# Input stage of a hybrid S5 and forgetting-attention block: norm weights spread by TensorE, memory's copies placed ahead of x's squares, one weight load moved forward

## The chip, the cores and the metric

The kernel runs on one core of one Trainium2 chip. The time is the device time of one execution in microseconds (us). A core has a matrix engine (TensorE, PE in the profile; its weight loads are PEld), VectorE (DVE), ScalarE (ACT), GpSimd (POOL) and SyncE (SP), which here only issues DMA transfers. Each engine runs its own instructions in a fixed order and waits on semaphores for the others. Tiles lie in SBUF (128 partitions); matrix products land in eight PSUM banks of 128x512 float32.

## What is computed

One decoder block over 1024 tokens of width 1024, with 256 memory tokens. The part that the change touches is the start: the normalised input, the normalised memory, its keys and values, and the first 512 columns of the input projection.

```python
def rms_norm(x, gain):
    xf = x.astype(jnp.float32)
    y = xf * lax.rsqrt(jnp.mean(xf * xf, axis=-1, keepdims=True) + RMS_EPS)
    return (y * gain.astype(jnp.float32)).astype(x.dtype)
...
    u = rms_norm(h, norm_mix[l])
    proj = u @ w_in[l]
    u_ssm, q, k, v, f_logit, gate_logits = jnp.split(proj, [...], axis=-1)
...
    # in the cross-attention
    k, v = jnp.split(rms_norm(mem, norm_mem_kv[l]) @ w_kv, 2, axis=-1)
```

After that come the state-space branch, forgetting attention, the gates, an output projection, the cross-attention, a SwiGLU FFN and a final norm. None of that code is changed.

## The kernel before

Every product is made in three passes of a fast float32 format: each operand is split into a high part (a cast copy on ACT, line 177) and a low part (source minus high part, line 178, on VectorE or for a few weights on GpSimd). `mm3` (lines 167 to 169) then runs high x high, high x low, low x high.

`stage_in` treats two memory tiles (`m`, `n`) and eight x tiles (`0` to `7`) of 128 tokens, and twelve weight pieces of 512 KB: 0 to 3 for the memory's keys, 4 to 7 for its values, 8 to 11 for the 512 columns of u. Its order is written out by hand in the string `ORDER_IN`, one short word a step; a scheduler then sets each engine's own order, starting from that string. The words:

- `F` loads a tile, `G` loads a norm weight spread over 128 partitions, `Q` squares a tile on ACT with a row sum, `R` makes the reciprocal root (VectorE, one power on GpSimd, VectorE), `S` scales the tile by root and norm weight on VectorE (`S3g`: ACT and GpSimd).
- `T` turns half a tile on TensorE into a PSUM bank (line 222), `E` copies the turned half out, split into high (`mh` or `uh`, ACT) and low (`ml` or `ul`, VectorE).
- `D` loads a weight piece (hexadecimal number), `W` splits it (`g`: low part on GpSimd), `K` and `V` are keys and values, `U` and `u` a product for u and its copy out, `Z` stores keys and values, `L` issues the small loads of the state-space parameters, `P` prepares these parameters, `X` issues that many warm-up products.

Three things in it matter for what follows. The turned halves use one bank of `misc` and two of `pv`, so a `misc` half can be turned only after the half before it has been copied out, both parts. The raw weights have few buffers (two `raw`, one `xraw`; the u pieces `wr` take tiles of the `xt` ring, that is of x tiles already turned), so a load can wait on SP for a split, and all loads behind it wait too. And ACT does squares, high parts and PSUM copies in one queue.

The norm weight comes in by one transfer that writes it to all partitions:

```python
    def gains(i):
        gain[i] = xtile("gain")
        S.dma_start(gain[i], (g_kv if i == 0 else g_mix).partition_broadcast(P))
```

Of the kernel before, what the change touches and what calls it, by code (L numbers as in the profile page):

```python
# [9 lines left out]
F32 = mybir.dt.float32  # L10
# [3 lines left out]
AF = mybir.ActivationFunctionType  # L14
# [5 lines left out]
P = 128  # L20
D = 1024
# [17 lines left out]
RSLOT_LATE = (0, 1, 2, 3, 4, 4, 5, 5, 6, 6, 7, 7)  # L39

ORDER_IN = """
G0 Fm Qm Fn D1 X60 Qn Rm D0 Sm F1 G1 Tm0 Rn Em0 Sn Tn0 F0 D2 Tm1 W0 Q0 Tn1 En0 F2 F3 D3 Q1 W1g En1 Em1 K0 F4 F5 K1 R0
S0 T00 T01 k0 E00 Q2 W2g D4 F6 F7 D8 E01 S1 T10 Q3 W3 k1 D5 K3 K2 W4 E10 W5 D6 R1 k2 T11 k3 S2 Q4 V0 S3g T30
E11 D7 Q5 T20 R2 T21 E21 E20 S4 E30 W6 D9 W7 T40 V1 S5 E40 T31 V2 E31 W8 T41 V3 Da Z0 L0 T50 Q6 v T51 W9
E51 U00 Db Z2 Q7 E41 R3 S6 u00 L1 Wa T60 E50 S7 T61 T70 Wbg E61 U10 E60 T71 E70 E71 P0 U20 u10 u20 P1 U21 U11 U30
P2 u30 U31 u11 u31 U01 u21 P3 P4 P5 u01
"""

# [18 lines left out]
def f32(ap):  # L67
    return ap.bitcast(F32)
# [50 lines left out]
class Block:  # L119
# [54 lines left out]
            self.mm3(ps, wh[:, k0 + k, :], wl[:, k0 + k, :], rh, rl, k == 0, k == nk - 1)  # L174

    def split(self, hi, lo, src, pool_lo=False):
        self.A.copy(hi, src)  # L177
        (self.G if pool_lo else self.V).tensor_sub(lo, src, f32(hi))  # L178

    def rstd(self, src):  # L180
# [111 lines left out]
def hybrid_block_kernel(ctx: ExitStack, tc: tile.TileContext, x, mem, norm_mix, w_in, b_forget,  # L292
# [22 lines left out]
    with tc.tile_pool(name="ssm", bufs=1) as sp:  # L315
        s5 = S5(B, sp, lam_re[0], lam_im[0], log_dt[0], b_re[0], b_im[0], c_re[0], c_im[0], d_skip[0])
        with tc.tile_pool(name="xin", bufs=1) as xp:
            stage_in(B, xp, s5, x, mem, norm_mix[0], norm_mem_kv[0], w_in, w_mem_kv, uT, u_d, kv_d)
        with tc.tile_pool(name="qp", bufs=1, reuse_waits="tile") as qp:
            stage_ssm(B, s5, qp, uT, w_in, gate_d, u_d, y_d, w_mix_out, sums_d)  # L320
# [13 lines left out]
def stage_in(B, xp, s5, x, mem, g_mix, g_kv, w_in, w_mem_kv, uT, u_d, kv_d):  # L334
# [5 lines left out]
    V, A, T, S, small = B.V, B.A, B.T, B.S, B.small  # L340
    junk = xp.tile([P, D], BF16, name="junk")
    mT = Act(xp, "mT", 4, 8, ML, kg=4, name="m")
    tiles, gain, ss, rs, raw, w, ps, us, kv = {}, {}, {}, {}, {}, {}, {}, [], []
    names = {"m": -2, "n": -1, **{str(t): t for t in range(NT)}}

    def xtile(name="xt"):
        return xp.tile([P, D], F32, tag="xt", bufs=12, name=name)

    def fetch(t):
        tiles[t] = xtile()  # L350
        S.dma_start(tiles[t], mem[(t + 2) * P:(t + 3) * P, :] if t < 0 else x[t * P:(t + 1) * P, :])

    def gains(i):
        gain[i] = xtile("gain")
        S.dma_start(gain[i], (g_kv if i == 0 else g_mix).partition_broadcast(P))

    def square(t):
        if t % 2 == 0:
            ss[t // 2] = small.tile([P, 2], F32, name="ss2")
        A.activation(junk, tiles[t], AF.Square, scale=1.0 / 32, accum_out=ss[t // 2][:, t % 2:t % 2 + 1])  # L360

    def root(i):
        rs[i] = B.rsqrt(ss[-1][:, i % 2:i % 2 + 1] if i < 0 else ss[i])
# [4 lines left out]
        B.norm_scale(tiles[t], tiles[t], r, gain[0 if t < 0 else 1], pool=pool)  # L368

    def turn(t, b):  # L370
        ps[t, b] = B.turn(tiles[t], b, ("misc", "pv")[b])

    def evac(t, b):
        B.turned(ps.pop((t, b)), b, *((mT, t + 2) if t < 0 else (uT, t)))
# [58 lines left out]
    def ssm_out(q, h):  # L433
# [4 lines left out]
        if h == 1:  # L438
            S.dma_start(u_d[q].rearrange("t p c -> p t c"), uv)

    prep = s5.prepare()

    acts = {"F": lambda a: fetch(names[a]), "G": lambda a: gains(int(a)), "Q": lambda a: square(names[a]),
            "R": lambda a: root(names[a]),
            "S": lambda a: scale(names[a[0]], a[1:] == "g"),
            "T": lambda a: turn(names[a[0]], int(a[1])), "E": lambda a: evac(names[a[0]], int(a[1])),
            "D": lambda a: wget(int(a, 16)), "W": lambda a: wsplit(int(a[0], 16), a[1:] == "g"),
            "K": lambda a: keys(int(a)), "k": lambda a: keys_out(int(a)), "V": lambda a: values(int(a)),
# [1461 lines left out]
```

## Time and profile before

| what | value |
|---|---|
| time, median of 3 runs | 1594.67 us |
| lowest and highest | 1586.8 and 1595.77 us |
| profiled execution, its own time | 1598.0 us |
| its span, first to last instruction | 1596.3 us |
| mean granted TensorE clock | 0.98 |
| bytes moved by DMA | 258.70 MB |

The profile shows one execution. Its page gives busy time by engine; other views of the same trace show one engine's instructions in order of time (start, duration, engine, line, operation, output<-input, count, and in brackets how long the engine had been idle and what ended that), the sum of waits by pair, and busy times in chosen stretches. An instruction of the memory stage is found by its line and tile names. The profiled execution is 3.3 us above the median of the runs.

### The profile page before, as it was taken

Reading aid. Unit: us, or ns where it says so; the run is one execution under the profiler, and the core shown is the slowest. Engines: PE = TensorE matmul, PEld = TensorE weight load, DVE = VectorE, ACT = ScalarE, POOL = GpSimd, SP = SyncE. Lnnn points to the kernel's source line nnn. Section 1 sums busy time; section 2 is a strip of 40 time slices with the busy share of each in tenths; the row PEclk is TensorE's granted clock in tenths of the full one; section 3 lists DMA queues with packets and bytes.
Section 4 is the critical chain, followed back from the end, with each engine's and each line's share of the span. In section 5 each row is a group of like instructions: output and inputs, shape, how many; then the busy total and the mean of one; then the engine's idle time right before and its main releaser. Section 6 shows DMA issues by size and latency. Waiting matters only on the chain.

```text
span 1596.3 us, 20515 instructions
## 1 busy us (share of the span) xinstructions
PE 1533.6 (96%) x7301; PEld 1261.0 (79%) x7301; DVE 1057.9 (66%) x1892; ACT 678.7 (43%) x1199; POOL 243.6 (15%) x323
## 2 busy tenths in 40 slices
PE   5899999999999899989999999999999999899997
PEld 5688888898777668878888778888888888688886
DVE  5756566444688676769765688677777775465455
ACT  5422334422566553434445564333333333244342
POOL 3015443200121123310002200000000000000001
PEclk8899999999999999999999999999999999999999
DMA  8745556752022736757531186544455544696542
GB/s 268 147 94 92 168 159 163 181 178 30 11 58 45 179 83 207 261 199 275 178 117 56 53 297 247 168 152 152 159 165 161 162 159 165 235 388 218 189 157 106
DMA packets 202870, 258.70 MB, mean 162 GB/s; under 512 B 36024, under 2 KB 127064, under 8 KB 202256
## 3 DMA queue, kind: packets, MB, share of 16 engines
q1 hardware_dynamic: 196144, 241.67, 50.5%
q10 hardware_dynamic: 6624, 15.73, 2.6%
q8 instruction: 57, 0.93, 0.2%
q14 instruction: 45, 0.37, 0.1%
HBM read 176.08 MB, written 83.20 MB: 162 GB/s over the span
## 4 chain that ended last, share of the span: by engine, by line
PE 72%; DVE 10%; DMA 8%; issue 3%; POOL 3%; ACT 3%; SPq 1%; DVEq 0%; ACTq 0%; POOLq 0%
PE mm L964 15%; PE pv L964 7%; PE mm L167 6%; PE mm L168 6%; PE mm L169 6%; PE mm L1101 4%; PE sc L964 4%; PE sc L1101 3%; PE pv L1101 3%; PE sc L167 2%; PE sc L169 2%; PE sc L168 2%; DMA or<-in_w_ffn_out_dram 1%; PE misc L1101 1%; DMA gb<-gate_d 1%
## 5 line engine op out<-in xcount | busy, mean ns | idle before, releaser
L178 DVE TENSOR_TENSOR wlo<-raw,whi 128x1024 fp32r<-128x1024 f32 (+2 forms) x126 | 133.7, 1063 | 104.7 <-ACT whi L177 104.2
L177 ACT CAST whi<-raw 128x1024 fp32r<-128x1024 f32 (+2 forms) x127 | 115.6, 914 | 140.8 <-PE mm L168 36.0
L167 PE MATMUL mm<-uh,whi 128*128 128x512 f32 x344 | 138.7, 403 | 2.2 <-ACT whi L177 2.2
L169 PE MATMUL mm<-uh,wlo 128*128 128x512 f32 x344 | 136.5, 397 | 0.2 <-DVE wlo L178 0.2
L178 DVE TENSOR_TENSOR ol<-or,oh 128x1024 fp32r<-128x1024 f32 x73 | 89.3, 1224 | 71.2 <-ACT oh L177 70.2
L168 PE MATMUL mm<-ul,whi 128*128 128x512 f32 x344 | 136.4, 397 | 0.0
L177 ACT CAST oh<-or 128x1024 fp32r<-128x1024 f32 x73 | 76.8, 1052 | 104.4 <-PE mm L1101 33.6
L996 POOL TENSOR_TENSOR g<-a,c 128x512 f32<-128x512 f32 x22 | 35.6, 1619 | 398.2 <-ACT a L995 398.2
L167 PEld LDWEIGHTS mm<-uh,whi 128*128 128x128 f32 x344 | 65.9, 192 | 14.8 <-ACT whi L177 2.6
L169 PEld LDWEIGHTS mm<-uh,wlo 128*128 128x128 f32 x344 | 65.6, 191 | 15.0 <-DVE wlo L178 1.4
L1729 POOL TENSOR_TENSOR pl<-pf,ph 128x512 fp32r<-128x512 f32 (+1 forms) x32 | 39.7, 1241 | 246.0 <-DVE ph L1728 200.4
L196 POOL TENSOR_TENSOR r<-ms,mhalf 128x1 f32<-128x1 f32 (+1 forms) x30 | 17.9, 599 | 376.9 <-DVE ms L192 347.4
L168 PEld LDWEIGHTS mm<-ul,whi 128*128 128x128 f32 x344 | 65.8, 191 | 11.0
L1726 ACT ACTIVATE pf<-sc 128x512 f32<-128x512 f32 (+1 forms) x96 | 46.5, 490 | 50.0 <-DVE sc L1722 30.4
L964 PE MATMUL pv<-S3h,we 128*128 128x512 f32 x176 | 58.1, 389 | 0.0
L1199 POOL TENSOR_TENSOR sg<-sg,ga 128x512 f32<-128x512 f32 x16 | 33.2, 2102 | 74.1 <-DVE sg L1192 30.1
L1732 DVE TENSOR_TENSOR pl<-pf,ph 128x512 fp32r<-128x512 f32 (+2 forms) x64 | 35.6, 557 | 11.6 <-ACT ph L1731 10.5
L1101 PE MATMUL mm<-oh 128*128 128x512 f32 x106 | 41.2, 389 | 0.0
L1101 PE MATMUL mm<-ol,oh 128*128 128x512 f32 x106 | 41.2, 389 | 0.0
L1101 PE MATMUL mm<-oh,ol 128*128 128x512 f32 x106 | 41.2, 389 | 0.0
L167 PE MATMUL mm<-yh,whi 128*128 128x512 f32 x104 | 41.1, 395 | 0.0
L169 PE MATMUL mm<-yh,wlo 128*128 128x512 f32 x104 | 40.9, 393 | 0.0
(681 smaller groups left out, 4589.5 us busy)
## 6 DMA issues: line engine op xcount, KB each, us to landing
or<-c_d SPq DMA_DIRECT2D x77, 256.0 KB
wo<-in_w_ffn_out_dram SPq DMA_DIRECT2D x22, 512.0 KB
c_d<-g SPq DMA_DIRECT2D x44, 256.0 KB
t_d<-wo SPq DMA_DIRECT2D x44, 256.0 KB
or<-t_d SPq DMA_DIRECT2D x44, 256.0 KB
raw<-in_w_ffn_in_dram SPq DMA_DIRECT2D x20, 512.0 KB
rawb<-in_w_ffn_in_dram SPq DMA_DIRECT2D x20, 512.0 KB
raw<-in_w_in_dram SPq DMA_DIRECT2D x18, 512.0 KB
```

Of the source, the lines that this page charges most:

```text
L167: T.matmul(ps, lh, rh, start=first, stop=False)
L168: T.matmul(ps, lh, rl, start=False, stop=False)
L169: T.matmul(ps, ll, rh, start=False, stop=last)
L177: self.A.copy(hi, src)
L178: (self.G if pool_lo else self.V).tensor_sub(lo, src, f32(hi))
L964: T.matmul(ps, l_[:, k, :], r_, start=first and k == 0 and i == 0, stop=k == 3 and i == 2, skip_group_check=True)
L996: G.tensor_mul(g[:, 512:], a1, c1)
L1101: T.matmul(ps, l_[:, gi], r_[:, 512:], start=n < 3 and p == 0 and k == 0 or n == 7 and p == 0 and k == 0, stop=p == NP - 1 and k == 2, ski ...
L1199: self.B.G.tensor_mul(self.out[j][:, cs], self.out[j][:, cs], ga)
L1726: self.exp = A.activation(pf[:, off:], ps[:, off:], AF.Exp)
L1729: G.tensor_sub(pl[:, off:], pf[:, off:], f32(ph[:, off:]))
L1732: V.tensor_sub(pl[:, off:], pf[:, off:], f32(ph[:, off:]))
```

## The change

The spread load of each norm weight is replaced. `G` now loads the 4 KB row into one partition (both rows first in the queue), and a new step `B` multiplies a column of ones with the row on TensorE, two products of 512 columns, and copies each from PSUM to the `gain` tile on ACT. In `ORDER_IN` both `G` stand first, `B0` behind the memory loads, `B1` behind all four memory copies. `B1`'s copies and the squares of x tiles 0 and 1 are ordered behind the last memory copy on ACT (`B.copied`, the last high part so far; `B.behind` only sets order). The first half of `n` is turned into a bank of `mm` in place of `misc`. The warm-up shrinks from 60 products to 12. `Db`, the load of the last u piece, moves ahead of `Z0 L0` (the key stores and small loads).

```diff
 ORDER_IN = """
-G0 Fm Qm Fn D1 X60 Qn Rm D0 Sm F1 G1 Tm0 Rn Em0 Sn Tn0 F0 D2 Tm1 W0 Q0 Tn1 En0 F2 F3 D3 Q1 W1g En1 Em1 K0 F4 F5 K1 R0
+G0 G1 Fm Fn B0 X12 Qm D1 Qn Rm D0 Sm F1 Tm0 Tm1 Rn Em0 Em1 Sn F0 D2 Tn0 Tn1 W0 En0 En1 B1 Q0 F2 F3 D3 Q1 W1g K0 F4 F5 K1 R0
...
-E11 ... V3 Da Z0 L0 T50 Q6 v T51 W9
+E11 ... V3 Da Db Z0 L0 T50 Q6 v T51 W9
-E51 U00 Db Z2 Q7 ...
+E51 U00 Z2 Q7 ...
...
     def split(self, hi, lo, src, pool_lo=False):
-        self.A.copy(hi, src)
+        self.copied = self.A.copy(hi, src)
...
+    ones = xp.tile([1, P], F32, name="ones")
+    V.memset(ones, 1.0)
+
     def gains(i):
+        row[i] = xp.tile([P, D], F32, tag="kv", bufs=4, name="row")[0:1, :]
+        S.dma_start(row[i], (g_kv, g_mix)[i].unsqueeze(0))
+
+    def gain_rows(i):
         gain[i] = xtile("gain")
-        S.dma_start(gain[i], (g_kv if i == 0 else g_mix).partition_broadcast(P))
+        for c in range(2):
+            cs = slice(512 * c, 512 * c + 512)
+            p_ = B.bank("sc")
+            T.matmul(p_, ones, row[i][:, cs], start=True, stop=True)
+            with B.behind(B.copied if i else None):
+                A.copy(gain[i][:, cs], p_)
...
-        A.activation(junk, tiles[t], AF.Square, scale=1.0 / 32, accum_out=ss[t // 2][:, t % 2:t % 2 + 1])
+        with B.behind(B.copied if t in (0, 1) else None):
+            A.activation(junk, tiles[t], AF.Square, scale=1.0 / 32, accum_out=ss[t // 2][:, t % 2:t % 2 + 1])
...
-        ps[t, b] = B.turn(tiles[t], b, ("misc", "pv")[b])
+        ps[t, b] = B.turn(tiles[t], b, "mm" if (t, b) == (-1, 0) else ("misc", "pv")[b])
```

Three places show how this moves instructions; everything behind the input stage keeps its order on every engine. First ACT at the program's start, before and then after (`junk` is the output of a square, `whi` a weight's high part, `mh` memory's turned halves, `kv` a key copy):

```order
L360 ACTIVATE junk,ss_119<-xt 128x1024 x2
L177 CAST whi<-raw 128x1024 x2
L360 ACTIVATE junk,ss_236<-xt 128x1024 x2
L177 CAST whi<-xraw 128x1024
L177 CAST mh_0_111<-misc 128x4x128
L360 ACTIVATE junk,ss_343<-xt 128x1024
L177 CAST mh_0_112<-pv 128x4x128 x2
L177 CAST mh_0_111<-misc 128x4x128
```

```order
L367 COPY gain<-sc 128x512 x2
L373 ACTIVATE junk,ss_145<-xt 128x1024 x2
L177 CAST mh_0_111<-misc 128x4x128
L177 CAST whi<-raw 128x1024
L177 CAST mh_0_112<-pv 128x4x128
L177 CAST whi<-raw 128x1024
L177 CAST mh_0_111<-mm 128x4x128
L177 CAST mh_0_112<-pv 128x4x128
L367 COPY gain<-sc 128x512 x2
L373 ACTIVATE junk,ss_215<-xt 128x1024
L177 CAST whi<-xraw 128x1024
L373 ACTIVATE junk,ss_215<-xt 128x1024
```

The four memory copies moved from behind two and three x squares to ahead of all of them, two PSUM copies stand in front of the first square and two more between memory's copies and x's squares.

Then GpSimd at the same place, before and after (`r` is a power of a reciprocal root: `r_315` before and `r_283` after belong to x tiles 0 and 1; `wlo` is a weight's low part; L214 scales x tile 3):

```order
L178 TENSOR_TENSOR wlo<-raw,whi 128x1024
L196 TENSOR_TENSOR r_315<-ms_314,mhalf 128x2
L178 TENSOR_TENSOR wlo<-xraw,whi 128x1024
L196 TENSOR_TENSOR r_441<-ms_440,mhalf 128x2
L196 TENSOR_TENSOR r_494<-ms_493,mhalf 128x2
L214 TENSOR_TENSOR xt<-xt,gain 128x1024
```

```order
L178 TENSOR_TENSOR wlo<-raw,whi 128x1024
L178 TENSOR_TENSOR wlo<-xraw,whi 128x1024
L196 TENSOR_TENSOR r_283<-ms_282,mhalf 128x2
L196 TENSOR_TENSOR r_409<-ms_408,mhalf 128x2
L214 TENSOR_TENSOR xt<-xt,gain 128x1024
```

The power for x tiles 0 and 1 moved behind the low part of weight piece 2.

Last SP's queue in the middle of the stage, before and after (`kv_d` is the store of keys; `prow`, `ldr`, `craw`, `b_re`, `b_im`, `dbc` are the small loads):

```order
L389 DMA wr<-in_w_in_dram 128x8x128 x2
L414 DMA kv_d<-kv 128x1024 x2
L1231 DMA prow<-in_lam_re_dram 16x128
L1232 DMA prow<-in_lam_im_dram 16x128
L1234 DMA ldr<-in_log_dt_dram 16x2
L1240 DMA craw<-in_c_re_dram 128x1x64 x4
L1240 DMA craw<-in_c_im_dram 128x1x64 x4
L1245 DMA b_re<-in_b_re_dram 128x16x16
L1245 DMA b_im<-in_b_im_dram 128x16x16
L1247 DMA dbc<-in_d_skip_dram 128x512
L389 DMA wr<-in_w_in_dram 128x8x128
L414 DMA kv_d<-kv 128x1024 x2
```

```order
L402 DMA wr<-in_w_in_dram 128x8x128 x3
L427 DMA kv_d<-kv 128x1024 x2
L1244 DMA prow<-in_lam_re_dram 16x128
L1245 DMA prow<-in_lam_im_dram 16x128
L1247 DMA ldr<-in_log_dt_dram 16x2
L1253 DMA craw<-in_c_re_dram 128x1x64 x4
L1253 DMA craw<-in_c_im_dram 128x1x64 x4
L1258 DMA b_re<-in_b_re_dram 128x16x16
L1258 DMA b_im<-in_b_im_dram 128x16x16
L1260 DMA dbc<-in_d_skip_dram 128x512
L427 DMA kv_d<-kv 128x1024 x2
```

The last u piece moved ahead of two stores and fourteen small loads.

More of the change, by code (lines that the diff above doesn't have):

```diff
@@ L41 @@
 ORDER_IN = """
-G0 Fm Qm Fn D1 X60 Qn Rm D0 Sm F1 G1 Tm0 Rn Em0 Sn Tn0 F0 D2 Tm1 W0 Q0 Tn1 En0 F2 F3 D3 Q1 W1g En1 Em1 K0 F4 F5 K1 R0
+G0 G1 Fm Fn B0 X12 Qm D1 Qn Rm D0 Sm F1 Tm0 Tm1 Rn Em0 Em1 Sn F0 D2 Tn0 Tn1 W0 En0 En1 B1 Q0 F2 F3 D3 Q1 W1g K0 F4 F5 K1 R0
 S0 T00 T01 k0 E00 Q2 W2g D4 F6 F7 D8 E01 S1 T10 Q3 W3 k1 D5 K3 K2 W4 E10 W5 D6 R1 k2 T11 k3 S2 Q4 V0 S3g T30
-E11 D7 Q5 T20 R2 T21 E21 E20 S4 E30 W6 D9 W7 T40 V1 S5 E40 T31 V2 E31 W8 T41 V3 Da Z0 L0 T50 Q6 v T51 W9
-E51 U00 Db Z2 Q7 E41 R3 S6 u00 L1 Wa T60 E50 S7 T61 T70 Wbg E61 U10 E60 T71 E70 E71 P0 U20 u10 u20 P1 U21 U11 U30
+E11 D7 Q5 T20 R2 T21 E21 E20 S4 E30 W6 D9 W7 T40 V1 S5 E40 T31 V2 E31 W8 T41 V3 Da Db Z0 L0 T50 Q6 v T51 W9
+E51 U00 Z2 Q7 E41 R3 S6 u00 L1 Wa T60 E50 S7 T61 T70 Wbg E61 U10 E60 T71 E70 E71 P0 U20 u10 u20 P1 U21 U11 U30
 P2 u30 U31 u11 u31 U01 u21 P3 P4 P5 u01
@@ L342, in stage_in @@
     mT = Act(xp, "mT", 4, 8, ML, kg=4, name="m")
-    tiles, gain, ss, rs, raw, w, ps, us, kv = {}, {}, {}, {}, {}, {}, {}, [], []
+    row, tiles, gain, ss, rs, raw, w, ps, us, kv = {}, {}, {}, {}, {}, {}, {}, {}, [], []
     names = {"m": -2, "n": -1, **{str(t): t for t in range(NT)}}
@@ L441, in stage_in @@
     prep = s5.prepare()
-    acts = {"F": lambda a: fetch(names[a]), "G": lambda a: gains(int(a)), "Q": lambda a: square(names[a]),
+    acts = {"F": lambda a: fetch(names[a]), "G": lambda a: gains(int(a)), "B": lambda a: gain_rows(int(a)), "Q": lambda a: square(names[a]),
             "R": lambda a: root(names[a]),
```

## The prediction

> **What bounds the kernel now.** I read the page first, then busy times by stretches of 10 us, then TensorE's waits, then the engines one by one around those waits. The page's first part says that TensorE is the bound:
>
> ```profile
> PE 1533.6 (96%) x7301; PEld 1261.0 (79%) x7301; DVE 1057.9 (66%) x1892; ACT 678.7 (43%) x1199; POOL 243.6 (15%) x323
> ```
>
> So a change of the input stage can only be worth time that TensorE loses there. The stretches (start:end, length, then busy us of each engine, granted clock, DMA share) show where that is:
>
> ```profile
> 0.00:10.00 10.00, 8.14 (x59) 6.61 (x60) 1.77 (x9) 3.58 (x5) 2.44 (x11) 1.00 0.82 256
> 10.00:20.00 10.00, 2.11 (x16) 1.37 (x13) 4.62 (x10) 6.52 (x9) 5.16 (x4) 0.79 1.08 366
> 20.00:30.00 10.00, 5.98 (x29) 5.58 (x30) 9.17 (x14) 5.96 (x12) 1.86 (x2) 0.53 1.04 336
> 30.00:40.00 10.00, 7.37 (x64) 7.17 (x62) 8.02 (x13) 6.86 (x13) 3.06 (x2) 0.98 0.44 116
> ...
> 60.00:70.00 10.00, 6.79 (x33) 5.07 (x31) 4.58 (x11) 3.60 (x8) 0.00 (x0) 1.00 1.00 215
> 70.00:80.00 10.00, 8.45 (x33) 6.53 (x34) 7.27 (x29) 2.92 (x7) 2.86 (x1) 0.66 0.33 69
> 80.00:90.00 10.00, 10.00 (x48) 8.25 (x48) 9.97 (x61) 2.57 (x6) 0.00 (x0) 1.00 0.01 2
> ```
>
> From 80 us TensorE is full (10.00 of 10). Before that it idles, its first 8.14 us are warm-up products, and at 20 to 30 and 70 to 80 it runs at a granted clock of 0.53 and 0.66, each time behind an idle stretch. Its waits up to 120 us:
>
> ```profile
> PE misc L222 <- DVE ml L178: 9.7, 1, 9.7
> PE misc L222 <- DVE ul L178: 4.7, 4, 2.7
> PE misc L1252 <- issue: 4.1, 1, 4.1
> ```
>
> The 9.7 us are memory's turned halves: the next `misc` half waits for the one before to be copied out, and ACT gets to that late. The 4.1 us are put down to nothing, so I followed the `misc` bank to ACT, whose rows on both places are:
>
> ```profile
> 6.43 1.06 ACT L360 ACTIVATE junk<-xt 128x1024 bf16<-128x1024 f32 x1 [4.35 <-DMA xt<-in_mem_dram]
> ...
> 17.68 1.03 ACT L177 CAST whi<-xraw 128x1024 fp32r<-128x1024 f32 x1
> 18.61 0.57 ACT L177 CAST mh<-misc 128x512 fp32r<-128x512 f32 x1
> ...
> 68.76 1.91 ACT L177 CAST whi<-wr 128x1024 fp32r<-128x1024 f32 x1 [5.36 <-DMA wr<-in_w_in_dram]
> ```
>
> At 68.76 ACT has stood 5.36 us for the last u piece. Behind it in the queue is the copy of a `misc` half that the parameters' transpose (L1252) needs. That load is issued late on SP, behind the small loads, the first of which is `prow`:
>
> ```profile
> 46.52 0.67 SPq L1231 DMA_DIRECT2D prow<-in_lam_re_dram  x1
> ...
> 58.94 0.38 SPq L389 DMA_DIRECT2D wr<-in_w_in_dram  x1
> ```
>
> TensorE's milestones, which the sum runs along (first key product, first product of V1, first u product, L1252, first product of the third u half, U20):
>
> ```profile
> 25.13 0.80 PE L167 MATMUL mm<-mh,whi 128*128 128x256 f32 x2 [0.68 <-ACT mh L177]
> ...
> 48.06 0.48 PE L167 MATMUL sc<-whi,mh 128*128 128x512 f32 x1
> ...
> 60.42 0.48 PE L167 MATMUL mm<-uh,whi 128*128 128x512 f32 x1
> ...
> 71.50 0.31 PE L1252 MATMUL misc<-ident,prow 48*128 48x48 f32 x1 [4.05 <-issue]
> ...
> 82.36 0.48 PE L167 MATMUL mm<-uh,whi 128*128 128x512 f32 x1
> ```
>
> **Part 1: norm weights by TensorE.** Two transfers of 512 KB go, two of 4 KB come. Memory tile `m` was second in the queue; at the 256 GB/s of the first stretch, 0.52 MB less brings it about 2 us before 6.43. What now stands ahead of its square: the row's landing, two products of 512 columns, two copies. No row shows the landing of so small a load at the start; it is between 2 us (issue at once, one us on the way) and 4.4 us (where `m` itself would land); I take 3.1. The products are plain float32; the nearest row is the 128-column one of the state-space output:
>
> ```profile
> L1503 PE MATMUL pv<-xg,Tt 128*128 128x128 f32 x64 | 12.4, 275 | 0.0
> ```
>
> 12.4/64 = 0.19 us, so 0.78 us for 512 columns at full clock, twice that at half. The granted clock of the first stretch reads 1.00, but in finer stretches (length, PE busy and count) the warm-up products run half as fast at first:
>
> ```profile
> 2.00:3.00 1.00, 1.00 (x6) 0.70 (x5) 0.00 (x0) 0.08 (x1) 0.00 (x0) 1.00 0.88 287
> ...
> 8.00:9.00 1.00, 1.00 (x11) 0.89 (x10) 0.48 (x3) 1.00 (x2) 0.93 (x4) 1.00 1.18 323
> ```
>
> 6 against 11 in one us, so I take half speed, 1.55 us each. The second copy (0.57 us for 512 columns, as the `mh` row) ends at 3.1 + 2 x 1.55 + 0.6 = 6.8. The first square then starts 0.3 us later than 6.43; by the bounds, 1.8 us earlier to 1.6 us later. The transfer saved is thus paid back on TensorE and ACT, and I cost this part at +0.3. A rule to weigh: the Trainium skill (TensorE: Matmul & The Clock Gate, "What's actually happening") says that TensorE runs at half clock until it has been busy for some 3.4 us, which agrees with 6 and 11 in the rows; by its opposite, a full clock from the start, this term would be 1.3 us earlier. The same section speaks against cutting the warm-up from 60 to 12; I price that in part 3.
>
> **Part 2: memory's copies ahead of x's squares.** Memory's tiles are scaled as before, 0.3 us later, so the last half is turned at about 13.3 us (four half tiles now have four banks, so none waits for another; the 9.7 us go). ACT then has four `mh` copies of 0.57 and two `whi` of 1.03 among them, done at 15; VectorE's low parts follow by 16.9. The first key product can run in full from 16.2 in place of 25.13: 9 us earlier.
>
> What pays for it is x. Behind memory's copies ACT does two gain copies (1.2), a square (1.06 and a short read of the sum, 1.2), a `whi` (1.03) and the second square: done at 19.4. GpSimd's order puts the power for these tiles behind the low part of weight piece 2:
>
> ```profile
> 18.05 0.70 POOL L196 TENSOR_TENSOR r<-ms,mhalf 128x2 f32<-128x2 f32 x1 [1.80 <-DVE ms L194]
> 18.78 2.38 POOL L178 TENSOR_TENSOR wlo<-xraw,whi 128x1024 fp32r<-128x1024 f32 x1
> ```
>
> That low part starts after its `whi` at 18.2 and takes 2.38, the power 0.70, three small steps 0.6: x tile 0 is scaled at 22.0, where it was 21.40. On SP, x tiles 2 to 5 now stand behind weight piece 3, which waits for the low part of piece 0 (15 us), so DMA idles some 2 us; their squares on ACT are due after 21 us, so I cost that at 0 (cover gone: 1 us).
>
> From there VectorE sets the pace up to weight piece 5 (`xraw`), which V1 needs:
>
> ```profile
> 21.40 1.28 DVE L216 SCALAR_TENSOR_TENSOR xt<-xt,r,gain 128x1024 f32<-128x1024 f32 x1
> 22.61 0.68 DVE L178 TENSOR_TENSOR ml<-misc,mh 128x512 fp32r<-128x512 f32 x1
> ...
> 43.88 1.21 DVE L178 TENSOR_TENSOR wlo<-xraw,whi 128x1024 fp32r<-128x1024 f32 x1
> ```
>
> Before, this stretch is 21.40 to 45.1, 23.7 us, of which some 17.9 are work (six scales at 1.2, four `ml` at 0.6, three `wlo` at 1.15, eight half-size subtractions at 0.34, small steps 2.2) and 5.8 are waits, much of them for the late keys. After, the order lists before the same row five scales (6.0), no `ml`, three `wlo` (3.4), twelve subtractions (4.1) and small steps (1.4): 14.9. With no wait at all piece 5 is ready at 36.9, with the old 5.8 at 42.7. I take 2.6 of waiting, since the keys are now early: 39.5, and V1 follows at 39.6 in place of 48.06: 8.5 us earlier.
>
> **Part 3: from V1 to the u products.** V1 to the first u product took 60.42 - 48.06 = 12.4. Its waits for turned halves (of the 4.7 above the longest, 2.7, lies earlier; two of the other three lie here, 1.3) shrink by 1.0. But TensorE has now idled some 4 us ahead of V1, and after idling the stretches above show about half clock; a stretch of 3.4 us at half loses 1.7. So 13.0, and the first u product is at 52.6, 7.8 us earlier than 60.42. Here the cut warm-up has its price too: without it the keys run at half clock for as long as before (0.53 at 20 to 30), which V1's wait for VectorE covers: 0; without that cover 1.7.
>
> **Part 4: the last u piece.** From the first u product to U20 took 82.36 - 60.42 = 21.9. ACT's 5.36 go, and with them the 4.05 of L1252 and the slow clock behind it: (1 - 0.66) x 8.45 = 2.9. In its place comes a shorter wait: the parameters' copy and the scales of x tiles 6 and 7 stand late on VectorE, so the `misc` bank turns over slowly around L1252; I take 0.9 us (0 to 3). So 15.9, and U20 stands at 68.5 in place of 82.4: 13.9 us earlier. On SP the load passes two stores and fourteen small loads; they start one issue (0.38) later at the same place of the queue, which itself is reached earlier, and nothing but L1252 and what follows it needs them: 0, as long as the load itself need not wait (below).
>
> **The sum.** x's scale comes 0.6 later (21.40 to 22.0, inside the next term), V1 8.5 earlier, the stretch to the first u product is 0.6 longer, the one to U20 6.0 shorter: -8.5 + 0.6 - 6.0 = -13.9 us, 14 rounded. From there TensorE is full and everything moves as one. The profiled execution took 1598.0, 3.3 above the median, so 1584.0 on its scale, and 1594.67 - 14 = 1580.7 as a median; I say 1581. About 1% (16 us) is what a measurement tells from no change.
>
> **Rivals.** *More than the sum:* VectorE works without a gap up to piece 5 (-2.6), the clock is full at V1 (-1.7), no new wait at L1252 (-0.9), and gain rows land early (-1.5): 20.7 us, 1574. For it: the waits were mostly for late keys. Against: ACT and VectorE copy each half in turns (high, low, high, low), which waits whatever the keys do.
>
> *Only the last piece counts:* x's scale is late by up to 3 us and VectorE waits as before (42.7 for piece 5 and later), V1 gains 3 or nothing and only the 4.05 + 2.9 of part 4 stay: about 7 to 9 us, 1587. For it: VectorE was 80 to 92% busy in the stretches from 20 to 40 us and loses only four `ml` and one scale.
>
> *Slower:* the moved load blocks SP. It takes a `wr` tile, so it waits for an x tile to be turned, and `prow`, `craw` and the others, once ahead of it, wait behind it. After the change L1252 needs them at 52.6 + (71.50 - 4.05 - 60.42) = 59.6 us, and they took 58.94 - 46.52 = 12.4 us to issue and some 2 to land; so from an issue at 45 us on, each us of waiting is a us lost, at 59 us the gain is gone, and at 62 us the time is 1598. Against it: the ring gives this load one of x tiles 0 and 1, which are turned among the keys' products, well before V1 at 39.6.
>
> **Chances.** The sum (gain of 10 to 18 us) 0.52, more than that 0.23, only the last piece 0.21, slower 0.04. More than 16 us of gain: the second and a fifth of the first, 0.33. A loss of over 16 us: at most 0.02. Within: 0.65. The range runs from the second case (1574) to the third (1587), each with a scatter of 2 to 3 us, since single runs lie 9 us apart: 1572 to 1590.
>
> **What would show it.** In the trace after: first square at 5 to 8 us; first key product before 18; x tile 0 scaled near 22; piece 5's low part done at 37 to 43 and V1 right behind; no idle ACT row on `wr`; U20 at 66 to 71. If V1 comes before 38 or U20 before 64, waits were sized too high; if `prow`'s transpose waits over 3 us on TensorE, part 4 is wrong; if the order from 80 us on shows new idle stretches, the shift was not passed on.

## The result, and the profile after

| | kernel before | changed kernel |
|---|---|---|
| first comparison, median | 1592.2 us (4 runs) | 1575.8 us (4 runs) |
| second comparison, median | 1590.5 us (9 runs) | 1579.1 us (5 runs) |
| ratio, with 95% interval | | 0.990 (0.988 to 0.992), then 0.993 (0.991 to 0.996) |
| profiled executions | 1598.0 and 1596.6 us | 1575.9 and 1579.1 us |

The changed kernel is 16.4 us faster in the first comparison and 11.4 in the second; its nine runs together have a median of 1577.2 us, about 14 us less than the kernel before, which lay between 1590.5 and 1593.2 in five comparisons. Predicted were 14 us less and 1581.

The page's first part for the changed kernel (busy us, share of the span, instructions):

```profile
PE 1524.9 (97%) x7261; PEld 1251.0 (79%) x7261; DVE 1055.2 (67%) x1893; ACT 680.2 (43%) x1203; POOL 239.3 (15%) x323
```

TensorE is busy 8.7 us less and still bounds the kernel. Only 2.8 of these us lie ahead of U20 (57.0 against 59.8); about 6 lie behind it, where its products are the same. The warm-up didn't get cheaper: 12 products and the row products take 9.9 us, the 60 products took 8.5. Busy times by stretches of 10 us (start:end, length, busy us of TensorE, its weight loads, VectorE, ScalarE and GpSimd, each with a count, then the granted clock, DMA share and GB/s):

```profile
10.00:20.00 10.00, 7.49 (x52) 6.07 (x51) 6.22 (x11) 6.92 (x12) 2.95 (x2) 1.00 0.67 224
20.00:30.00 10.00, 8.13 (x55) 7.72 (x54) 7.56 (x16) 7.70 (x16) 3.81 (x3) 0.83 1.01 352
...
60.00:70.00 10.00, 8.57 (x47) 6.61 (x47) 9.65 (x51) 2.92 (x8) 0.00 (x0) 1.00 0.95 219
70.00:80.00 10.00, 10.00 (x46) 8.26 (x45) 10.00 (x48) 1.63 (x4) 0.00 (x0) 1.00 0.03 10
```

At 10 to 20 us TensorE is busy for 7.49 in place of 2.11, at 20 to 30 the clock is 0.83 in place of 0.53, and TensorE is full from 70 us on, one stretch earlier than before. The milestones of the prediction, in TensorE's rows:

```profile
2.44 7.16 PE L365 MATMUL sc<-row,ones 1*128 1x512 f32 x8 [2.44 <-DMA row<-in_norm_mem_kv_dram]
9.53 2.74 PE L240 MATMUL misc<-ident 128*128 128x256 bf16 x12
12.33 0.71 PE L222 MATMUL misc<-ident,xt 128*128 128x128 f32 x4
...
17.31 0.39 PE L168 MATMUL mm<-ml,whi 128*128 128x256 f32 x1 [0.22 <-DVE ml L178]
...
40.27 0.73 PE L167 MATMUL sc<-whi,mh 128*128 128x512 f32 x2 [0.45 <-ACT whi L177]
41.75 0.50 PE L168 MATMUL sc<-wlo,mh 128*128 128x512 f32 x1 [0.75 <-DVE wlo L178]
...
54.37 0.48 PE L167 MATMUL mm<-uh,whi 128*128 128x512 f32 x1
60.01 0.26 PE L1265 MATMUL misc<-ident,prow 48*128 48x48 f32 x1
...
69.82 0.47 PE L167 MATMUL mm<-uh,whi 128*128 128x512 f32 x1
```

Keys with their low parts run from 17.31 (before 26.44), V1 starts at 40.27 (48.06), the first u product is at 54.37 (60.42), the parameters' transpose waits for nothing (4.05), and U20 is at 69.82 (82.36). ScalarE and VectorE around them:

```profile
6.71 1.06 ACT L373 ACTIVATE junk<-xt 128x1024 bf16<-128x1024 f32 x1
...
39.17 1.05 ACT L177 CAST whi<-xraw 128x1024 fp32r<-128x1024 f32 x1 [1.27 <-DMA xraw<-in_w_mem_kv_dram]
...
53.04 1.98 ACT L177 CAST whi<-wr 128x1024 fp32r<-128x1024 f32 x1
```

```profile
24.11 2.48 DVE L216 SCALAR_TENSOR_TENSOR xt<-xt,r,gain 128x1024 f32<-128x1024 f32 x2
...
40.48 1.22 DVE L178 TENSOR_TENSOR wlo<-xraw,whi 128x1024 fp32r<-128x1024 f32 x1
```

ScalarE no longer stands before the last u piece (its row at 53.04 shows no wait). But ahead of V1 it stands 1.27 us for the landing of weight piece 5 (`xraw`), whose high part is done at 40.22, and VectorE comes to the low part at 40.48: two chains end there almost together. This became the main question.

### The profile page after: what moved, and what is told of

Read it like the earlier page. It is cut to its first block, busy times and chain, and to the rows that moved or that the text cites. A ratio compares the mean times of both kernels' runs of the same rounds, so it can differ in the third digit from the quotient of the medians.

```text
span 1574.2 us, 20451 instructions
## 1 busy us (share of the span) xinstructions
PE 1524.9 (97%) x7261; PEld 1251.0 (79%) x7261; DVE 1055.2 (67%) x1893; ACT 680.2 (43%) x1203; POOL 239.3 (15%) x323
## 4 chain that ended last, share of the span: by engine, by line
PE 77%; DVE 8%; DMA 7%; ACT 3%; issue 2%; POOL 2%; SPq 1%; DVEq 0%; POOLq 0%; ACTq 0%
PE mm L977 15%; PE pv L977 8%; PE mm L167 6%; PE mm L168 6%; PE mm L169 6%; PE mm L1114 5%; PE sc L977 4%; PE sc L1114 4%; PE pv L1114 3%; PE sc L167 2%; PE sc L169 2%; PE sc L168 2%; PE misc L1114 2%; DMA gb<-gate_d 1%; PE mm L627 1%
## 5 line engine op out<-in xcount | busy, mean ns | idle before, releaser
L167 PEld LDWEIGHTS mm<-uh,whi 128*128 128x128 f32 x344 | 65.4, 190 | 15.5 <-ACT whi L177 3.5
L167 PE MATMUL sc<-uh,whi 128*128 128x512 f32 x104 | 40.8, 392 | 0.0
```

The lines of the kernel that those rows point to most:

```text
L167: T.matmul(ps, lh, rh, start=first, stop=False)
```

## Experiments

All times are of the same quantities: first key product with a low part, first u product, U20, the stretch between these two (each from one profile), and the median of the runs. Profile and median belong to different executions: for both profiles of the kernel before, for the last piece back, the bank, no warm-up and x tiles ahead, the profiled execution took 3 to 6 us more than the median, for the others within 0.6 us of it.

| kernel | key | first u | U20 | u to U20 | median us | ratio to before |
|---|---|---|---|---|---|---|
| before | 26.4 | 60.4 | 82.4 | 21.9 | 1592.2 | 1 |
| before again | 26.5 | 61.3 | 84.2 | 22.9 | 1590.5 | 1 |
| changed | 17.3 | 54.4 | 69.8 | 15.5 | 1575.8 | 0.990 (0.988 to 0.992) |
| changed again | 17.9 | 57.4 | 72.7 | 15.3 | 1579.1 | 0.993 (0.991 to 0.996) |
| before + last piece forward | 26.5 | 62.3 | 78.2 | 15.9 | 1585.1 | 0.997 (0.995 to 0.999) |
| changed, last piece back | 17.7 | 57.1 | 78.3 | 21.2 | 1584.9 | 0.997 (0.995 to 0.998) |
| before + bank of mm | 24.2 | 57.9 | 80.6 | 22.7 | 1587.7 | 0.997 (0.995 to 0.999) |
| changed, spread loads | 15.8 | 55.4 | 74.1 | 18.7 | 1578.1 | 0.992 (0.990 to 0.993) |
| changed, copies behind x | 19.0 | 59.4 | 75.0 | 15.7 | 1581.8 | 0.994 (0.992 to 0.996) |
| changed, squares' steps first | 17.6 | 57.9 | 73.3 | 15.4 | 1582.0 | 0.994 (0.992 to 0.996) |
| changed, no warm-up | 16.2 | 55.4 | 70.6 | 15.2 | 1577.1 | 0.992 (0.989 to 0.995) |
| changed, x tiles ahead | 17.6 | 61.8 | 79.9 | 18.0 | 1582.5 | 0.995 (0.993 to 0.998) |
| both of the last two | 16.1 | 56.7 | 72.5 | 15.8 | 1578.3 | 0.992 (0.990 to 0.994) |
| no warm-up, piece 5 ahead | 16.1 | 54.3 | 70.0 | 15.7 | 1577.0 | 0.991 (0.988 to 0.995) |

**The last piece alone, on the kernel before.** Its load moved forward, nothing else:

```diff
-T41 V3 Da Z0 L0 T50 ... E51 U00 Db Z2
+T41 V3 Da Db Z0 L0 T50 ... E51 U00 Z2
```

> Kernel before with one edit: the load of the last u piece stands ahead of the key stores and small loads; all other engines keep their order but for one copy on ScalarE. Theory (two separate gains): V1 stays at 48 us and the first u product at 60.4; ScalarE no longer stands 5.4 us for that piece, the 4.05 us ahead of the parameters' transpose go to under 1, and U20 comes at about 76 in place of 82.4, so the time is about 1586 against 1592 before. Rival (the last piece is the whole gain): U20 at 70 to 71, time 1580. Rival (another wait ends the same place): the transpose waits for its small loads instead, U20 at 80 or later, time 1590 or more.

The stretch from the first u product to U20 fell from 21.9 to 15.9, the transpose waited 0.65, and 6.5 us went in time. U20 came at 78.2 and not at 76, since the stretches ahead of it were 1 to 2 us later than in the first profile of before; in its second they are 0.9 later. Against that one U20 is 6.0 earlier. The other wait did not come.

**The last piece put back, in the changed kernel.** The same edit the other way round.

> Changed kernel with the load of the last u piece put back behind the small loads. Theory (two separate gains): first u product stays at 54.4, the wait for the last piece costs its 6.5 us again, U20 at about 76, time about 1582. Rival (the two parts need each other): SyncE issues the small loads no earlier than before (46 to 47 us in both traces), so the last piece is issued at about 59 and lands at about 69 whatever the keys do; then U20 is back at 81 to 83 and the time at 1588 to 1592, and early keys alone are worth nothing.

ScalarE's row shows the wait again:

```profile
65.95 1.98 ACT L177 CAST whi<-wr 128x1024 fp32r<-128x1024 f32 x1 [6.78 <-DMA wr<-in_w_in_dram]
```

The stretch is back at 21.2 and the time at 1584.9. The first u product came at 57.1 and not at 54.4, near the second profile of the changed kernel. U20 at 78.3 lies between the two forecasts. SyncE issued the load at 55.8 and not at 58.9, so all the rest of the change is worth 4 to 6 us at U20 and 6.7 in time without the last piece, not nothing. The two parts add: 6.5 and 6.7 make 13.2, and the changed kernel has 11.4 and 16.4 in its two comparisons.

**The bank alone, on the kernel before.** The first half of tile `n` goes to a bank of `mm`:

```diff
-        ps[t, b] = B.turn(tiles[t], b, ("misc", "pv")[b])
+        ps[t, b] = B.turn(tiles[t], b, "mm" if (t, b) == (-1, 0) else ("misc", "pv")[b])
```

> Kernel before with one edit of the change: the first half of memory tile n is turned into a bank of mm in place of misc, so that no half waits for another's copy (spread loads, 60 warm-up products, the squares ahead on ScalarE and the last piece's place as before; the scheduler moves copies of turned x halves up). Theory: ScalarE still reaches memory's copies at 18.6 us, behind the squares of x tiles that land at 15.4, and VectorE their low parts at 22.6, so the 9.7 us wait goes but the first full key product comes at 23 to 25 in place of 26.4; V1 at 44 to 47; with the wait for the last u piece still there U20 stays at 80 to 84, time within 3 us of before. Rival (the shared bank alone held the keys): first full key product at 21 or earlier, V1 at 43 or earlier.

```profile
24.23 0.56 PE L168 MATMUL mm<-ml,whi 128*128 128x256 f32 x1
...
42.37 0.48 PE L167 MATMUL sc<-whi,mh 128*128 128x512 f32 x1
```

In the TensorE rows above (keys, then V1) the keys gain 2.2 us, as the theory had it, yet V1 comes at 42.37, as the rival had it: 5.7 us earlier than before, without early keys. With the bank free the scheduler also puts the copies of x's turned halves earlier on ScalarE. At U20 1.8 us of it are left against the first profile of before and 3.6 against the second, because ScalarE then stands 8.06 us for the last u piece:

```profile
68.33 1.91 ACT L177 CAST whi<-wr 128x1024 fp32r<-128x1024 f32 x1 [8.06 <-DMA wr<-in_w_in_dram]
```

In time the edit is worth 0.3% (0.1 to 0.5%), 5.5 us between the medians; the 3 us expected at most lie within that interval. With the 6.5 us of the last piece alone that makes 12 of about 14. No run has these two edits without the rest of the change; so what norm weights by TensorE, the new order on ScalarE and the shorter warm-up add is some 2 us by subtraction, inside the scatter, and not shown.

**Norm weights loaded spread again.** `gains` as in the kernel before, `B0 B1` left out, `G1` behind `F1`:

```diff
-        row[i] = xp.tile([P, D], F32, tag="kv", bufs=4, name="row")[0:1, :]
-        S.dma_start(row[i], (g_kv, g_mix)[i].unsqueeze(0))
+        gain[i] = xtile("gain")
+        S.dma_start(gain[i], (g_kv, g_mix)[i].partition_broadcast(P))
```

> Changed kernel with both norm weights loaded spread over 128 partitions again (two transfers of 512 KB, no row products, no PSUM copies); memory's copies, the 12 warm-up products and the last piece's load as in the changed kernel. Theory 1 (the prediction's: part 1 pays for itself): DMA stands idle some 4 us at 12 to 16 us in the changed kernel, so 1 MB more fills that hole and delays little; memory's turns no longer wait behind 7.2 us of row products; first full key product at 15.5 to 18, U20 within 2 us of 69.8. Theory 2 (part 1 is what makes room): x tiles 0 and 1 and weight pieces land 3 us later; U20 at 72.5 or later, time 1579 or more. In the time theory 1 says 1575 to 1578.

Keys came 1.5 us earlier than in the changed kernel, as expected without the row products, and the 1 MB did fill the idle DMA (its share is 1.08 at 13 to 16 us). U20 at 74.1 is as theory 2 had it, 1.4 to 4.3 later than in the two profiles of the changed kernel, and the transpose waits 1.0 us again; the time, 1578.1, lies between the theories. The scheduler moved other instructions with the edit, so some 1 us of time, inside the scatter, is all that can be said for part 1.

**Memory's copies forced behind x's squares.**

```diff
-Sm F1 Tm0 Tm1 Rn Em0 Em1 Sn F0 D2 Tn0 Tn1 W0 En0 En1 B1 Q0 F2 F3 D3 Q1 W1g
+Sm F1 Tm0 Tm1 Rn Sn F0 D2 Tn0 Tn1 W0 Q0 Q1 Em0 Em1 En0 En1 B1 F2 F3 D3 W1g
...
-        with B.behind(B.copied if t in (0, 1) else None):
-            A.activation(
+        if True:
+            B.squared = A.activation(
...
+        with B.behind(B.squared if t < 0 else None):
```

> Changed kernel with memory's four copies put behind the squares of x tiles 0 and 1 on ScalarE by force, as they stood before; loads by rows, banks and the last piece's load as in the changed kernel (the scheduler also moves three small loads on SyncE). Theory O (the order on ScalarE gave the early keys, as the prediction's part 2 had it): copies wait for x as before, first full key product at 21 or later, V1 at 44 or later, U20 at 73 or later, time 1579 or more. Theory L (the landing of x tile 1 gave them): in the kernel before ScalarE stood in that queue for x tiles that landed at 15 to 16.6 us; with 1 MB less ahead of them both have landed by about 12, their squares fit into ScalarE's gap at 9 to 13 us, first full key product is at 18 or earlier and x tile 0 is even scaled earlier than 24.1; U20 within 1.5 us of 69.8 or ahead of it.

```profile
12.76 1.06 ACT L373 ACTIVATE junk<-xt 128x1024 bf16<-128x1024 f32 x1 [0.68 <-DMA xt<-in_x_dram]
...
13.95 1.06 ACT L373 ACTIVATE junk<-xt 128x1024 bf16<-128x1024 f32 x1
...
15.00 0.57 ACT L177 CAST mh<-misc 128x512 fp32r<-128x512 f32 x1
```

ScalarE's rows show x's squares at 12.8 and 14.0, where the kernel before had them at 15.4 and 16.6, so memory's copies start at 15.0 and keys at 19.0, only 1.7 us later than in the changed kernel. With the loads by rows, the order on ScalarE is thus 1.7 of the 9.1 us by which keys came earlier; the bank alone gave 2.2, and the rest goes with the earlier landing of x's tiles. The run with spread loads, where the order stayed and keys came at 15.8, is the other side of it: either edit frees memory's copies from the wait for x. Keys fit neither theory (18 or earlier, 21 or later). V1 at 42.1 is short of theory O's 44, but U20 at 75.0 and the time fit it: x tiles 2 to 7 had moved on SyncE behind weight pieces 3 and 4 and three small loads, ScalarE stood 2.3 us for one of them at 23.7, and V1 waited 4.05. So the run tells of the keys and not of the end.

**The squares' steps first in the order string.**

```diff
-Sm F1 Tm0 Tm1 Rn Em0 Em1 Sn F0 D2 Tn0 Tn1 W0 En0 En1 B1 Q0 F2 F3 D3 Q1 W1g
+Sm F1 Tm0 Tm1 Rn Sn F0 D2 W0 Q0 Em0 Em1 Tn0 Tn1 F2 F3 D3 Q1 W1g En0 En1 B1
...
-            with B.behind(B.copied if i else None):
+            if True:
...
-        with B.behind(B.copied if t in (0, 1) else None):
+        if True:
```

> Changed kernel with part 2 taken back as far as the order string does it: squares of x tiles 0 and 1 and their norm weight's copies in their old places among memory's copies, no instruction tied behind memory's last copy. Theory: VectorE sets the way to V1, and with late keys it waits between; first full key product at 21 or later, V1 at 45 to 48, first u product at 58 to 60, U20 at 74 to 76, time about 1581. Rival: x scaled earlier makes up for late keys; V1 within 2 us of 40.3 and U20 within 2 us of 69.8, time 1576.

This did not do what it was for. The scheduler kept memory's copies ahead of the squares without being told to, so keys stayed at 17.6. What it changed was the place of the loads of x tiles 2 and 3, ahead of weight piece 3, as in a run below, and the order on ScalarE, where three squares stand ahead of the high part of weight piece 2 (22.4 in place of 18.9). V1 came at 42.5 and U20 at 73.3, outside both forecasts; the time, 1582.0, is the theory's. x tiles 0 and 1 were scaled at 21.3, 2.9 us earlier than in the changed kernel, and V1 still came 2.3 later: scaling x earlier did not bring V1 forward. With this string the ties of the change (`B.behind`) were not needed to keep memory's copies in front.

**No warm-up, and x tiles ahead of piece 3.** The first drops `X12`, with the order of the other engines unchanged. The second moves two loads:

```diff
-F0 D2 Tn0 Tn1 W0 En0 En1 B1 Q0 F2 F3 D3 Q1
+F0 D2 F2 F3 Tn0 Tn1 W0 En0 En1 B1 Q0 D3 Q1
```

> Changed kernel without the 12 warm-up products that are left; the order on the other four engines is the same. Theory: memory's turned halves wait on TensorE behind the row products and the warm-up (12.33 us, scale of the first memory tile done at 10.6), so without it the first turn is at 10.7, first full key product at 15.7 in place of 17.3, x tiles 0 and 1 scaled 1 to 1.6 us earlier, U20 at 68.3 to 69. Rival: the clock is granted later, keys run at half speed for 3.4 us, but VectorE still sets V1: U20 at 69.8 with no change. Rival, loss: U20 at 71 or later since the half-clock stretch lies on the path. In the time 1 to 1.5 us, no more than the scatter of runs.

> Changed kernel with the loads of x tiles 2 and 3 ahead of weight piece 3 on SyncE, so that they fill the 4 us in which DMA stands idle at 12 to 16 us (piece 3 waits there for a raw buffer). Theory D (weight piece 5's landing, through a full DMA queue, sets V1): the landing of piece 5 moves from 39.2 to 36 to 37, V1 from 40.3 to 38 or earlier, U20 to 67 to 68.5, time 1574 to 1575. Theory V (VectorE's chain of scales and low parts sets V1): V1 stays at 39.5 to 40.5 and U20 within 1 us of 69.8, the idle DMA costs nothing, as the prediction priced it.

> Changed kernel with x tiles 2 and 3 ahead of weight piece 3 as well as without the 12 warm-up products. Without them alone the turns came at 10.74 and x tile 0 was scaled 1.2 us earlier, but piece 5 landed 1 us later and U20 did not move. Theory (VectorE and piece 5's landing are tied ahead of V1, each must be moved): both together bring V1 to 38 to 38.5 and U20 to 67 to 68, 2 us more than either alone. Rival (scatter of the DMA queue covers it): U20 at 69 to 71.

Without the warm-up the turns start at 10.74, keys 1.1 us earlier, and U20 does not move: piece 5 lands later and TensorE waits 2.65 us for it. Neither time nor U20 shows a loss by the clock. With the x tiles ahead, DMA is full at 13 to 16 us, but a buffer is free later: SyncE issues piece 5 at 25.95 in place of 22.50 and the next two pieces at 32.07 in place of 27.75, TensorE waits 3.7 us for a key weight's low part, and DMA idles in part at 28 to 40. First the changed kernel, then this one:

```profile
13.00:16.00 3.00, 1.35 (x13) 1.11 (x11) 2.23 (x4) 2.92 (x5) 0.00 (x0) 1.00 0.22 57
...
28.00:32.00 4.00, 4.00 (x30) 4.00 (x29) 3.42 (x10) 2.53 (x6) 0.70 (x1) 0.81 0.99 228
32.00:36.00 4.00, 4.00 (x29) 3.64 (x28) 3.41 (x7) 3.97 (x10) 2.39 (x1) 1.00 0.90 171
36.00:40.00 4.00, 2.55 (x17) 1.87 (x15) 3.09 (x8) 2.58 (x5) 0.70 (x2) 1.00 0.95 248
```

```profile
13.00:16.00 3.00, 1.65 (x15) 1.42 (x13) 1.97 (x3) 2.62 (x4) 0.00 (x0) 1.00 1.07 376
...
28.00:32.00 4.00, 0.34 (x3) 0.14 (x2) 4.00 (x4) 3.13 (x6) 2.35 (x1) 1.00 0.71 128
32.00:36.00 4.00, 3.94 (x24) 3.94 (x25) 3.13 (x11) 1.92 (x5) 0.69 (x1) 0.69 0.56 183
36.00:40.00 4.00, 4.00 (x23) 3.52 (x22) 2.51 (x5) 2.40 (x8) 0.00 (x0) 0.88 0.35 106
```

DMA's share (last but one column) goes from 0.22 to 1.07 in the first row and from 0.99, 0.90, 0.95 to 0.71, 0.56, 0.35 in the others. Both theories fell: V1 came at 41.3, and U20 at 79.9 in a profile that took 6.3 us more than the median. But the idle DMA is not what made the loads late. With the two loads the scheduler also moved squares of x on ScalarE: three stand ahead of piece 2's high part, where the changed kernel has one. GpSimd's low part follows it, and piece 5 takes the `xraw` tile that this frees. ScalarE and SyncE in the changed kernel, then here:

```profile
18.90 1.09 ACT L177 CAST whi<-xraw 128x1024 fp32r<-128x1024 f32 x1
...
22.50 2.98 SPq L402 DMA_DIRECT2D xraw<-in_w_mem_kv_dram  x1
```

```profile
21.70 1.07 ACT L177 CAST whi<-xraw 128x1024 fp32r<-128x1024 f32 x1
...
25.95 0.38 SPq L402 DMA_DIRECT2D xraw<-in_w_mem_kv_dram  x1
```

So the run doesn't tell what filling the idle DMA is worth by itself. Both edits together gave 72.5, later than either forecast. V1 is at 41.3 in that run too; the 7.4 us between the two come behind it, where ScalarE stood 3.6 us for a u piece in one and not in the other, and the medians are 4.2 us apart. Single profiles of this stage scatter by several us.

**No warm-up, and piece 5's load ahead of the first u piece.**

```diff
-G0 G1 Fm Fn B0 X12 Qm
+G0 G1 Fm Fn B0 Qm
...
-F6 F7 D8 E01 S1 T10 Q3 W3 k1 D5 K3
+F6 F7 E01 S1 T10 Q3 W3 k1 D5 D8 K3
```

> Changed kernel without the 12 warm-up products and with weight piece 5's load ahead of the first u piece's (D8 behind D5; the scheduler moves some copies on ScalarE with it). Without the warm-up alone VectorE was 1.9 us early for piece 5, ScalarE stood 3.5 us for its landing and TensorE 2.7. Theory (piece 5's landing through the full DMA queue is what sets V1 there): ScalarE's wait for it goes under 1 us, V1 comes at 39 or earlier in place of 41.3, first u product at 53.5 or earlier, U20 at 67.5 to 69. Rival (the wait moves on: the first u piece lands later and the copies behind it are late): U20 at 70 to 72.

```profile
35.45 0.73 PE L167 MATMUL sc<-whi,mh 128*128 128x512 f32 x2
...
38.99 0.50 PE L168 MATMUL sc<-wlo,mh 128*128 128x512 f32 x1 [2.81 <-DVE wlo L178]
...
54.25 0.48 PE L167 MATMUL mm<-uh,whi 128*128 128x512 f32 x1
```

V1 starts at 35.45, 4.8 us earlier than in the changed kernel and 5.8 earlier than without the warm-up alone, so the landing was what held its start. Then TensorE waits 2.81 for its low part, which VectorE reaches only after two scales, ScalarE stands 2.55 for piece 6 at 38.76, and by the first u product the gain has gone (54.25 against 54.37). The wait moved on, as the rival said, and U20 at 69.95 is next to its 70. At 1577.0 this kernel is level with the changed kernel's 1577.2.

**Both kernels again, unchanged.**

> Kernel before, unchanged, for a second profile. After 80 us every kernel run so far gains a further 4 to 12 us on the one profile of before. Theory A (that profile was one of the slow executions; the later stages are the same code in the same order): a second profile has U20 at 82 to 83, the lead of the changed kernel at U20 is 12 to 13 us again, and its end lies 3 us or more ahead of the first one's 1596.3. Theory B (the changed kernel also saves time after 80 us): the second profile ends at 1595 to 1598 with the same waits at 239 and 1367 us.

> Changed kernel, unchanged, for a second profile and more runs. Theory: V1 at 40 to 41.5 (it hangs on a landing through a full DMA queue, which scattered by 1 us between like kernels), U20 at 69 to 71, from there the same order without new idle stretches, time 1575 to 1577. Rival (the first profile was a lucky one): U20 at 72 or later, time 1578 or more.

The second profile of the changed kernel shows how one landing scatters. ScalarE and TensorE:

```profile
41.18 1.04 ACT L177 CAST whi<-xraw 128x1024 fp32r<-128x1024 f32 x1 [4.02 <-DMA xraw<-in_w_mem_kv_dram]
```

```profile
42.28 1.22 PE L167 MATMUL sc<-whi,mh 128*128 128x512 f32 x2 [2.76 <-ACT whi L177]
```

Piece 5 comes 2.0 us later than in the first (SyncE had issued its load 0.5 later, at 23.00), V1 as well, a half-clock stretch follows, and U20 is at 72.7. So the first profile was on the lucky side, as the rival said (72 or later, 1578 or more). The kernel before came out nearer to theory B: its second profile ends 1.4 us earlier, at 1594.9, with U20 1.8 us later and both waits there, somewhat shorter (0.7 in place of 0.9 us near 240, 2.7 in place of 3.3 near 1368). Between U20 and the end, where all kernels have the same order, lie 1513.9 and 1510.7 us in the two profiles of before, 1504.4 and 1504.6 in those of the changed kernel, and 1502 to 1510 in the other ten. But both profiled executions of before are some 6 us above its medians: by 1591.6, the middle one of these, less 1.7 around the span and 83.3 for U20 (as in its two profiles), its usual rest is 1506.6, as in the others. The wait near 240 is in neither profile of the changed kernel; a gain behind U20 beyond it is not shown, and what makes that scatter stays open.

## Why the prediction was right, and where it was not

**Part 1, +0.3 us.** Right for the first square (6.71, forecast 6.8), by two errors that cancel: the row landed at 2.44 and not at 3.1, but the two products and copies took 4.4 us in place of 3.7. (At full clock the same sum ends at 5.3, that is 1.5 us earlier and not 1.3.) Not seen was that the row products (7.16 us, sized at 6.2) and the warm-up behind them hold TensorE until 12.3 us, 1.6 after tile `m` is ready. In the run without warm-up x tile 0 was scaled 1.2 us earlier for it and U20 was not; the run with spread loads puts the whole part at 1 us or so, inside the scatter.

**Part 2, V1 at 39.6.** V1 came at 40.27 and 42.28. Keys came at 17.3, 1.1 us behind the forecast. x tiles 0 and 1 were scaled at 24.1 in place of 22.0: with memory's turns late, ScalarE came late to piece 2's high part, and GpSimd's low part of it, which their power stands behind, started at 20.06 and not at 18.2. VectorE's stretch from there to piece 5's low part was sized right, 17.6 us against 17.5. That V1 is only 0.7 late is luck: its first products need the high part alone, and the first one with the low part is at 41.75, 2.2 behind. Of the 5.8 us of waits that the prediction took from the old stretch, 2.2 were no wait for keys. They are one short step of the reciprocal root (0.16 us elsewhere), which started and ended together with GpSimd's scale of x tile 3. VectorE and GpSimd in the kernel before:

```profile
32.49 2.35 DVE L200 TENSOR_TENSOR rt<-r 128x2 f32<-128x2 f32 x1 [0.80 <-POOL r L196]
...
32.42 2.41 POOL L214 TENSOR_TENSOR xt<-xt,gain 128x1024 f32<-128x1024 f32 x1
```

In the changed kernel that scale holds up a step by 0.4 us only, so the shorter waits, near the 2.6 forecast, are not owed to early keys alone. And of the 9.7 us that the prediction puts on ScalarE, the last 4 were VectorE's: the high part was done at 19.2, the low part begun at 22.6, behind x tile 0's scale. The step that failed is "from there VectorE sets the pace up to weight piece 5". Piece 5's landing through a full DMA queue does so as much: its high part was done 0.3 us before VectorE came to it in one profile, and VectorE waited 2.0 us for it in the other. With its load issued ahead of the first u piece's, V1 started at 35.45. And the early keys, on which the step rested, were not what V1 needed: the bank alone, with keys at 24.2, brought it to 42.4. The idle DMA, priced at 0, was 3 us and not 2 (its share is 0.01 from 14 to 17 us). The run with spread loads filled it and U20 gained nothing; the runs with x tiles ahead changed more than that.

**Part 3, 13.0 us.** It took 14.1 and 15.1. This term was sized too small. "Its waits for turned halves shrink by 1.0" is wrong: they were 0.55 and 0.87 before and 1.08 and 1.03 after, and V1 itself waits 0.75 for its low part. The half-clock stretch, taken as 3.4 us and priced at 1.7, did not come in the first profile. In the second it came with the long wait ahead of V1 and lasted 6.8 us, some 6 of them on V1's products, which by the same reckoning loses 3.0:

```profile
40.00:44.00 4.00, 1.68 (x3) 0.96 (x4) 2.00 (x4) 2.82 (x6) 0.00 (x0) 0.68 0.98 162
44.00:48.00 4.00, 4.00 (x13) 3.12 (x13) 3.38 (x6) 3.39 (x4) 0.00 (x0) 0.50 1.06 185
```

**Part 4, 15.9 us.** Right, and for its reasons: 15.45 and 15.34 in the changed kernel, 15.87 where this part was done alone, 21.2 where it alone was undone. The new wait around the parameters' transposes, put at 0.9, is 0.9 in both profiles, with a wait of 0.5 and 0.3 for an x tile's scale ahead of it. The moved load did not block SyncE: the small loads start 0.6 us later than before (47.12), and the transpose does not wait for them.

**The sum.** Forecast -13.9 at U20; measured -12.5 between the first profiles and -12.0 as the mean over two profiles each. Part 2 gave 0.7 less than forecast in the first profile, part 3 another 1.1, part 4 0.4 more. In time it is 14 us, so the sum held, within a scatter of some 3 us at U20 between the two profiles; that is 0.7% and 1.0% in the two comparisons, at and under the bound of 1%. That the time gained 2 us more than U20 is not explained. *More than the sum* did not come: the waits it left out were there. *Only the last piece counts* is refuted by the run that undid it: the rest is worth 6.7 us by itself, and the bank alone, on the kernel before, gave 5.5.

## What to carry to other kernels

Where two edits free two waits in a row, undo each alone: here the bank brought V1 5.7 us forward and U20 only 1.8 to 3.6 as long as the later one (a late load) stayed, and milestones of the trace showed it where the time alone could not. When a stage becomes short enough, its loads can be what ends last; ask then which buffer a load waits for, and which engine frees it. Moving two loads of x here also moved x's squares on ScalarE, and with them the moment at which the next weight's buffer came free. So look at every engine's order before a run is read as a test of one edit. An estimate of a few us in such a stage should carry the scatter of one landing, here 2 us in two profiles of the same program.

## What the runs showed of the hardware

**Row products do not raise TensorE's clock.** In the changed kernel TensorE is busy without a gap for 7 us on products with one row of contraction. Finer stretches, two of these, then one of the warm-up behind them:

```profile
2.50:5.90 3.40, 3.40 (x4) 1.38 (x5) 0.00 (x0) 0.59 (x1) 0.10 (x1) 1.00 0.95 315
5.90:9.30 3.40, 3.40 (x5) 0.97 (x3) 0.63 (x4) 2.78 (x5) 0.56 (x1) 1.00 1.16 316
9.50:12.30 2.80, 2.77 (x13) 1.64 (x12) 2.03 (x6) 0.00 (x0) 0.55 (x1) 1.00 1.02 378
```

Four or five a stretch, no faster in the second. Then the 12 warm-up products take 2.74 us, as long as the same 12 take in the run with spread loads, where nothing stands ahead of them:

```profile
1.86 2.74 PE L240 MATMUL misc<-ident 128*128 128x256 bf16 x12 [1.86 <-POOL ident masks.py:199]
```

That is the slow rate of the prediction's rows (6 in one us, counting those cut by its edges, against 11 later). By the Trainium skill (TensorE: Matmul & The Clock Gate, "What's actually happening") some 3.4 us of sustained activity end the half clock; these rows do not agree for products of one row. The clock column reads 1.00 throughout and shows nothing of it.

**A full DMA can move half as much.** Share and GB/s in the changed kernel, from stretches ahead of and among the u pieces' loads:

```profile
24.00:28.00 4.00, 2.80 (x16) 2.60 (x17) 3.96 (x6) 2.02 (x5) 0.00 (x0) 0.77 0.99 363
...
44.00:48.00 4.00, 3.90 (x19) 2.95 (x17) 3.53 (x4) 3.35 (x4) 0.00 (x0) 1.00 1.07 196
```

```profile
DMA packets 524, 1.45 MB, mean 363 GB/s; under 512 B 45, under 2 KB 45, under 8 KB 523
```

```profile
DMA packets 1876, 0.99 MB, mean 198 GB/s; under 512 B 25, under 2 KB 1867, under 8 KB 1874
```

The packet lines are of 24 to 28 and of 42 to 47 us: 2.8 KB a packet in the first, 0.5 KB in the second, at the same share (0.99). The u pieces, of 128 columns each, come in such small packets, and one of them stands ahead of pieces 5 and 6 in SyncE's order.
